# When a layer's input features are loaded and summed at the start of an encoder kernel: x's loads behind later weights, its sums behind later value chunks, the narrow projection one chunk later, the first k-tile in halves

## The chip, the core and the metric

The kernel runs on one core of a Trainium2 chip. A core has TensorE (matrix products, called PE in the profile; its weight loads are PEld), VectorE (DVE), ScalarE (ACT), GpSimd (POOL) and SyncE (SP), which here only issues transfers. Sixteen DMA engines move data between the chip's main memory and the core's own. The metric is the time of one execution on the device in microseconds, lower is better; a measurement is the median of several runs.

## What is computed

One layer of a streaming encoder, in float32: 256 tokens of 2048 features. A mixer (retention and a gated delta rule, both from one projection `w_in` of the normalised input), cross-attention into 256 memory tokens, and an MLP, with a residual addition after each and a final norm. What the change touches is the beginning of the work:

```
h = rms_norm(x, norm_mix_g)            # h1 in the kernel: input of every w_in projection
proj = h @ w_in                        # its 32 columns ga, gb give decays and betas of the delta rule
...
mem_n = rms_norm(mem, norm_mem_g)
k, v = split(mem_n @ w_xkv, 2)         # keys and values of the cross-attention
```

The norm of mem divides each token by a number of its own, so the kernel multiplies mem by the gain first, starts the products at once, and applies the per-token factor to the results later.

## The kernel before

Every product of two float32 matrices is made of three: each operand is split into a rounded part (hi, made by ScalarE with a copy into the narrower format) and a rest (lo, made by VectorE: the value less hi), and hi·hi + hi·lo + lo·hi are added up. So each piece of weights is loaded by a DMA into a `raw` buffer (three of them), cast to `whi` on ScalarE (L117) and `wlo` on VectorE (L118), half a megabyte at a time, and then used by TensorE. `fetch` (L95) does this; its instructions have a high priority. Activations are kept the same way, in quads of four k-tiles (128 features each): `memq` for mem, `h1` for the normalised x.

The kernel is written with a scheduler: it orders each engine's instructions by priority and data, when the program is built. On the chip each engine then runs its own list strictly in order, and a DMA is issued by the engine on whose list it stands. A transfer uses one of a few semaphores, and an issue waits until the earlier transfer that used the same one has landed.

The start of the program, in the order of the text:

- Eight calls of a matmul on ones warm TensorE up (L243, `WARM`). ScalarE issues the load of `gains` (L239), the gains of four norms.
- `values_both` (L363) makes the first two of four 512-column chunks of the values v together, k-tile by k-tile. Here block (q, n) is four k-tiles 4q to 4q+3 of chunk n; a block is 24 matmuls. For q = 0, `fetch_both` (L336) loads the weights in single k-tiles (L343), each with its k-tile of mem (L319), and casts them (L355, L358); `round_memory` splits mem times its gain into the quad, hi on ScalarE (L325), lo on VectorE (L326). For q = 1 to 3, mem is loaded by `load_memory` ahead of the block's weights, and rounded in the text behind the casts of the block's weights. TensorE's products are L370 to L372.
- `values(2)` and `values(3)` make the third and fourth chunk with the general `chunk` (L145, products L158 to L160). `keep_values` copies a result out of TensorE's memory (L333) and stores it.
- `narrow` (L211) makes the 32 columns of `w_in` with `h1`, 16 matmuls (L223), between the third and the fourth chunk, and `decay_rows` (L497) turns them into the decay rows `crow`, with a long chain of small VectorE instructions and some transposes on TensorE (L504, L544).
- Eight key blocks follow (L589 on, `blocks`, products L200 and L201), and beside them `rows_of`, `decays` and `ret_decays` prepare tables that the mixer reads later.

Beside this runs a generator `early` (L445), advanced by one `yield` for every two k-tiles of TensorE's products (`step`). The q = 0 blocks make steps 1 to 4, (1,0) 5 and 6, (1,1) 7 and 8, (2,0) 9 and 10, and so on to 16; the third chunk makes steps 17 to 24, the fourth 25 to 32. `behind()` (L79) orders what is traced inside it after the latest cast of weights on ScalarE and VectorE and after the latest load of weights on SP, if it runs on the same engine. Before the change `early` does the following: at steps 5 and 6 ScalarE issues the four loads of x (L452, half a megabyte each); at step 7 ScalarE issues `small` and `posi` (L456, L457); at steps 9 to 12 come the sums of squares of x (`norm_of`: squares on ScalarE L290, additions on VectorE L292 and L299, then the row of factors, which takes VectorE, GpSimd, TensorE and ScalarE in turn); at steps 13 to 20 `h1` (L468, L125, L126), one eighth a step; at steps 21 to 24 the sums of mem; then the rotations (VectorE, L413 to L441).

Of the kernel before, what the change touches and what calls it, by code (L numbers as in the profile page):

```python
# [17 lines left out]
P = 128  # L18
D = 2048
# [29 lines left out]
WARM = 8  # L49
# [3 lines left out]
def trunk(ctx: ExitStack, tc: tile.TileContext, x_f, mem_f, positions, gains_f, small_f, w_in, ret_gn_g, w_out, w_xq,  # L53
# [182 lines left out]
    with tc.high_priority(offset=300000):  # L236
        vec.memset(ones, 1.0)
        vec.memset(warm, 0.0)
        act.dma_start(gains, gains_f)  # L239
# [74 lines left out]
    mem_f32 = []  # L314

    def load_memory(c, ks):
        if ks.start == 0:
            mem_f32.append(kv.tile([P, 4, S], F32, name="xc", tag="xc", bufs=8))
        nc.sync.dma_start(mem_f32[c][:, ks], mem_f[:, 4 * c + ks.start:4 * c + ks.stop])  # L319

    def round_memory(c, ks):
        qh, ql = memq[c]
        for k in range(ks.start, ks.stop):
            g = gains[:, G_MEM + 4 * c + k:G_MEM + 4 * c + k + 1]
            act.activation(qh[:, k, :], mem_f32[c][:, k], AF.Copy, scale=g)  # L325
            vec.scalar_tensor_tensor(ql[:, k, :], mem_f32[c][:, k], g, qh[:, k, :].bitcast(F32),  # L326
                                     op0=ALU.mult, op1=ALU.subtract)
# [8 lines left out]
    def fetch_both():  # L336

        raws = [wp.tile([P, 2048], F32, name="raw", tag="raw", bufs=3) for _ in range(2)]
        got = []
        with tc.high_priority(offset=100000):  # L340
            for k in range(4):
                for n in range(2):
                    fetched.append(nc.sync.dma_start(raws[n][:, k * 512:(k + 1) * 512],  # L343
                                                     w_xkv[0, k * P:(k + 1) * P, D + n * 512:D + n * 512 + 512]).ins)
                    if not n:
                        load_memory(0, slice(k, k + 1))
            for h in range(2):
                tiles = [[wp.tile([P, 1024 + room], F32R, name=nm, tag=nm, bufs=3)[:, :1024]
                          for nm, room in (("whi", 64), ("wlo", 0))] for _ in range(2)]
                for k in range(2):  # L350
                    cs = slice(k * 512, (k + 1) * 512)
                    for n in range(2):
                        src = raws[n][:, (2 * h + k) * 512:(2 * h + k + 1) * 512]
                        hi, lo = (a[:, cs] for a in tiles[n])
                        latest["hi"] = act.activation(hi, src, AF.Copy).ins  # L355
                        if not n:
                            round_memory(0, slice(2 * h + k, 2 * h + k + 1))
                        latest["lo"] = vec.tensor_sub(lo, src, hi.bitcast(F32)).ins  # L358
# [4 lines left out]
    def values_both():  # L363
        pss = [stream_ps() for _ in range(2)]

        def products(n, kk, w, i):
            for t in range(NT):
                xh, xl = (a[:, kk % 4, t * P:(t + 1) * P] for a in memq[kk // 4])
                wh, wl = (a[:, i, :] for a in w)
# [823 lines left out]
```

## Time and profile before

| | |
|---|---|
| median of 3 runs | 2074.87 us (2074.64 to 2077.21) |
| the profiled execution | 2072.99 us |
| its span, first to last instruction | 2071.3 us |
| TensorE busy | 2057.7 us, 99% |
| VectorE busy | 1421.8 us, 69% |
| ScalarE busy | 1096.4 us, 53% |
| moved by DMA | 405.09 MB, mean 196 GB/s |

The page's second part cuts the span into 40 slices of 52 us; this change lies in the first two. A group line gives source line, engine, operation, what is written and read, shape and count, then busy time and mean duration in ns, then the engine's idle time before it and what ended it. A timeline row gives start, duration, engine, line and tiles, and in brackets the idle time before; several alike are merged, with their count. "q" behind an engine's name is its instruction queue, where DMA issues stand. A row of the waits gives who waited for whom, the total, how often and the longest. A row of the windows gives the stretch, its length, the busy time and count of each engine, the granted clock, the mean share of the DMA engines and GB/s. In TensorE's rows a duration includes the way through the array, so successive matmuls overlap, and the distance of their starts is the better measure.

### The profile page before, as it was taken

The numbers are of one execution on the slowest core, as the hardware profiler recorded it, in microseconds if no ns is written. First come the engines' busy times: TensorE is split into PE (matmuls) and PEld (weight loads), VectorE is DVE, ScalarE is ACT, GpSimd is POOL, SyncE is SP. The second block draws the span as 40 slices with busy tenths as digits, with TensorE's granted clock in tenths as the row PEclk, the third lists the DMA queues.
The fourth block names the chain that finished last, engine by engine and source line by source line (L and its number), as shares of the span: only waits on it lengthen the run. The fifth ranks groups of instructions, "written<-read, shape, count | busy, mean of one in ns | idle before, by whom it ended". The sixth has DMA issues, their size and how long they took to land.

```text
span 2071.3 us, 28351 instructions
## 1 busy us (share of the span) xinstructions
PE 2057.7 (99%) x10952; PEld 1773.0 (86%) x10952; DVE 1421.8 (69%) x2259; ACT 1096.4 (53%) x1739; POOL 30.6 (1%) x37
## 2 busy tenths in 40 slices
PE   9999999999999999999999999999999999999998
PEld 7788888988888888888888899888888888888887
DVE  6967778779767875888567665776556556655654
ACT  6655764675456554755455555554444434434444
POOL 0000000000000000000000000000000000000000
PEclk9999999999999999999999999999999999999999
DMA  8688566556556565655567654688666556656654
GB/s 295 209 286 270 177 195 197 162 183 186 187 171 190 181 194 163 190 182 178 163 223 237 191 183 143 191 209 231 199 187 192 195 190 196 185 201 186 197 187 142
DMA packets 329078, 405.09 MB, mean 196 GB/s; under 512 B 35040, under 2 KB 239088, under 8 KB 328816
## 3 DMA queue, kind: packets, MB, share of 16 engines
q1 hardware_dynamic: 327648, 400.34, 61.9%
q10 hardware_dynamic: 1296, 2.95, 0.4%
q8 instruction: 85, 1.39, 0.3%
q14 instruction: 49, 0.40, 0.1%
HBM read 389.61 MB, written 11.55 MB: 194 GB/s over the span
## 4 chain that ended last, share of the span: by engine, by line
PE 97%; DMA 1%; DVE 1%; ACT 0%; issue 0%; SPq 0%; ACTq 0%; POOLq 0%; POOL 0%; DVEq 0%
PE s L200 33%; PE s L201 17%; PE s L159 13%; PE s L158 13%; PE s L160 13%; DMA raw<-w_xkv 1%; PE b L760 1%; PE b L667 1%; PE b L793 1%; PE b L130 0%; PE b L129 0%; PE b L131 0%; PE s L372 0%; PE s L370 0%; PE s L371 0%
## 5 line engine op out<-in xcount | busy, mean ns | idle before, releaser
L118 DVE TENSOR_TENSOR wlo<-raw,whi 128x1024 fp32r<-128x1024 f32 x696 | 850.8, 1223 | 496.8 <-ACT whi L117 489.3
L117 ACT ACTIVATE whi<-raw 128x1024 fp32r<-128x1024 f32 x696 | 736.8, 1060 | 702.3 <-PE s L160 349.6
L200 PE MATMUL s<-q,whi 128*128 128x512 f32 x3072 | 1057.1, 391 | 0.3 <-DVE q L1060 0.3
L201 PE MATMUL s<-q,wlo 128*128 128x256 f32 x3072 | 838.7, 281 | 0.4 <-DVE wlo L118 0.4
L200 PEld LDWEIGHTS s<-q,whi 128*128 128x128 f32 x3072 | 567.4, 188 | 110.2 <-DVE q L1060 0.5
L201 PEld LDWEIGHTS s<-q,wlo 128*128 128x128 f32 x3072 | 576.4, 188 | 13.5 <-DVE wlo L118 1.1
L159 PE MATMUL s<-wlo,q 128*128 128x512 f32 (+1 forms) x1200 | 470.2, 392 | 0.0
L160 PE MATMUL s<-whi,q 128*128 128x512 f32 (+1 forms) x1200 | 467.6, 390 | 0.0
L158 PE MATMUL s<-whi,q 128*128 128x512 f32 (+1 forms) x1200 | 427.8, 390 | 0.0
L158 PEld LDWEIGHTS s<-whi,q 128*128 128x128 f32 x1200 | 225.0, 188 | 47.2
L160 PEld LDWEIGHTS s<-whi,q 128*128 128x128 f32 x1200 | 225.4, 188 | 45.8
L159 PEld LDWEIGHTS s<-wlo,q 128*128 128x128 f32 x1200 | 225.5, 188 | 45.3
L207 ACT ACTIVATE bo<-s 128x256 f32<-128x256 f32 x192 | 72.7, 379 | 124.4 <-PE s L201 111.3
L208 DVE TENSOR_TENSOR bo<-bo,s 128x256 f32<-128x256 f32 x192 | 80.0, 417 | 44.5 <-ACT bo L207 44.2
L620 DVE SCALAR_TENSOR_TENSOR acc<-bo,small,acc 128x255 f32<-128x255 f32 (+1 forms) x144 | 66.8, 480 | 3.1 <-ACT acc L617 1.2
L729 DVE TENSOR_TENSOR pr<-lw,tw 32x31 f32<-32x31 f32 (+15 forms) x124 | 40.5, 326 | 7.9 <-DMA lw<-scr_l 5.8
L731 DVE TENSOR_TENSOR tw<-tw,pr 32x31 f32<-32x31 f32 (+15 forms) x124 | 40.6, 327 | 2.0
L1107 DVE SCALAR_TENSOR_TENSOR res<-s,rstd3q,res 128x512 f32<-128x512 f32 (+1 forms) x32 | 22.3, 735 | 11.9 <-PE s L160 11.9
L894 ACT ACTIVATE gth<-s 128x512 f32<-128x512 f32 x32 | 18.9, 591 | 17.9 <-PE s L160 15.2
L1094 DVE SCALAR_TENSOR_TENSOR hs<-bo 128x256 f32<-128x256 f32 x64 | 26.9, 421 | 1.1
L1097 DVE TENSOR_TENSOR q<-hs,q 128x256 fp32r<-128x256 f32 x64 | 26.7, 419 | 0.0
L370 PE MATMUL s<-whi,q 128*128 128x512 f32 x64 | 23.4, 410 | 3.2 <-ACT q L325 3.2
(307 smaller groups left out, 1176.4 us busy)
## 6 DMA issues: line engine op xcount, KB each, us to landing
raw<-w_in SPq DMA_DIRECT2D x143, 1024.0 KB
raw<-w_ff SPq DMA_DIRECT2D x128, 1024.0 KB
raw<-w_xkv SPq DMA_DIRECT2D x29, 1024.0 KB
raw<-w_out SPq DMA_DIRECT2D x16, 1024.0 KB
raw<-w_xq SPq DMA_DIRECT2D x16, 1024.0 KB
raw<-w_xo SPq DMA_DIRECT2D x16, 1024.0 KB
dec_d<-dec_w SPq DMA_DIRECT2D x8, 384.0 KB
dec<-dec_d SPq DMA_DIRECT2D x8, 384.0 KB
```

Source lines behind the costliest of these rows:

```text
L117: latest["hi"] = act.activation(hi[:, cs], src[:, cs], AF.Copy).ins
L118: latest["lo"] = vec.tensor_sub(lo[:, cs], src[:, cs], hi[:, cs].bitcast(F32)).ins
L158: pe.matmul(o, xh, wh, start=first, stop=False)
L159: pe.matmul(o, xh, wl, start=False, stop=False)
L160: pe.matmul(o, xl, wh, start=False, stop=last)
L200: pe.matmul(ps[b], lh, xhl, start=kk == 0, stop=False)
L201: pe.matmul(ps[b][:, :S], ll, xh, start=False, stop=kk == KT - 1)
L207: act.activation(o, ps[b][:, S:], AF.Copy)
L208: vec.tensor_add(o, o, ps[b][:, :S])
L620: vec.scalar_tensor_tensor(acc[:, d:], ps[:, :S - d], cw[:, j, blk:blk + 1], acc[:, d:], op0=ALU.mult, op1=ALU.add)
L729: vec.tensor_mul(pv, lw[:, j, j + 1:32].unsqueeze(2).to_broadcast([32, n, j + 1]), tw[:, j, 0:j + 1].unsqueeze(1).to_broadcast([32, n, j + ...
L731: vec.tensor_sub(tw[:, j + 1:32, 0:j + 1], tw[:, j + 1:32, 0:j + 1], pv)
```

## The change

- **x's loads.** `early` yields eight times before it loads x, one chunk a step (steps 9 to 12), and SP issues the loads, `small` and `posi` as well (step 13), with a second load of mem's first k-tile, which the sums of mem need.
- **The sums.** Four more yields follow, so the sums of x come at steps 17 to 20, in the third value chunk, `h1` at steps 21 to 24, a quarter a step, the sums of mem at steps 25 to 28 and the rotations at step 29.
- **mem.** The loads of mem's third and fourth quad are traced behind the weights of blocks (1,1) and (2,0), and the rounding of a quad ahead of the block's fetch, behind the casts of the block before.
- **The first k-tile.** One load `lead`, issued by ScalarE, brings the gains and mem's first k-tile together. VectorE makes that k-tile's hi part (`first_q`). The first 512 columns of weights are loaded, cast and multiplied in two halves of 256. `WARM` is 6 instead of 8. The gains are copied from `lead` to their own tile later.
- **The narrow projection** comes behind the fourth chunk. `rows_of` moves into the third key block, and `decays` are spread over the key blocks from the fourth on.
- `trimask` is made in place, without `zer`.

```diff
@@ -46,11 +46,11 @@
-WARM = 8
+WARM = 6
...
@@ -236,7 +236,6 @@
     with tc.high_priority(offset=300000):
         vec.memset(ones, 1.0)
         vec.memset(warm, 0.0)
-        act.dma_start(gains, gains_f)
         act.activation(warm, warm, AF.Exp)
         early = bank()
         for _ in range(WARM):
@@ -312,19 +311,26 @@
     kv.tile([P, PAD1], F32, name="pad1", bufs=1)
     memq = [new_quad(kv, 4) for _ in range(4)]
     mem_f32 = []
+    lead = kv.tile([P, 64 + S], F32, name="lead", bufs=1)
+    mem_0 = lead[:, 64:]
+    with tc.high_priority(offset=400000):
+        act.dma_start(lead, lead_f)
+    with tc.high_priority(offset=300000):
+        first_q = vec.tensor_scalar(memq[0][0][:, 0, :], mem_0, lead[:, G_MEM:G_MEM + 1], None, op0=ALU.mult).ins
 
     def load_memory(c, ks):
-        if ks.start == 0:
+        if len(mem_f32) == c:
             mem_f32.append(kv.tile([P, 4, S], F32, name="xc", tag="xc", bufs=8))
-        nc.sync.dma_start(mem_f32[c][:, ks], mem_f[:, 4 * c + ks.start:4 * c + ks.stop])
+        return nc.sync.dma_start(mem_f32[c][:, ks], mem_f[:, 4 * c + ks.start:4 * c + ks.stop])
 
     def round_memory(c, ks):
         qh, ql = memq[c]
         for k in range(ks.start, ks.stop):
-            g = gains[:, G_MEM + 4 * c + k:G_MEM + 4 * c + k + 1]
-            act.activation(qh[:, k, :], mem_f32[c][:, k], AF.Copy, scale=g)
-            vec.scalar_tensor_tensor(ql[:, k, :], mem_f32[c][:, k], g, qh[:, k, :].bitcast(F32),
-                                     op0=ALU.mult, op1=ALU.subtract)
+            src = mem_f32[c][:, k] if c or k else mem_0
+            g = lead[:, G_MEM + 4 * c + k:G_MEM + 4 * c + k + 1]
+            if c or k:
+                act.activation(qh[:, k, :], src, AF.Copy, scale=g)
+            vec.scalar_tensor_tensor(ql[:, k, :], src, g, qh[:, k, :].bitcast(F32), op0=ALU.mult, op1=ALU.subtract)
 
     def keep_values(n, ps):
         vo = kv.tile([P, NT, 512], F32, name="vo", tag="vo", bufs=2)
@@ -337,25 +343,32 @@
 
         raws = [wp.tile([P, 2048], F32, name="raw", tag="raw", bufs=3) for _ in range(2)]
         got = []
+
+        def halves(n, k):
+            return ((0, 256), (256, 512)) if n == k == 0 else ((0, 512),)
+
         with tc.high_priority(offset=100000):
             for k in range(4):
                 for n in range(2):
-                    fetched.append(nc.sync.dma_start(raws[n][:, k * 512:(k + 1) * 512],
-                                                     w_xkv[0, k * P:(k + 1) * P, D + n * 512:D + n * 512 + 512]).ins)
-                    if not n:
+                    for c0, c1 in halves(n, k):
+                        at = D + n * 512
+                        fetched.append(nc.sync.dma_start(raws[n][:, k * 512 + c0:k * 512 + c1],
+                                                         w_xkv[0, k * P:(k + 1) * P, at + c0:at + c1]).ins)
+                    if n == 0 and k:
                         load_memory(0, slice(k, k + 1))
             for h in range(2):
                 tiles = [[wp.tile([P, 1024 + room], F32R, name=nm, tag=nm, bufs=3)[:, :1024]
                           for nm, room in (("whi", 64), ("wlo", 0))] for _ in range(2)]
                 for k in range(2):
-                    cs = slice(k * 512, (k + 1) * 512)
                     for n in range(2):
-                        src = raws[n][:, (2 * h + k) * 512:(2 * h + k + 1) * 512]
-                        hi, lo = (a[:, cs] for a in tiles[n])
-                        latest["hi"] = act.activation(hi, src, AF.Copy).ins
-                        if not n:
-                            round_memory(0, slice(2 * h + k, 2 * h + k + 1))
-                        latest["lo"] = vec.tensor_sub(lo, src, hi.bitcast(F32)).ins
+                        for c0, c1 in halves(n, 2 * h + k):
+                            src = raws[n][:, (2 * h + k) * 512 + c0:(2 * h + k) * 512 + c1]
+                            hi, lo = (a[:, k * 512 + c0:k * 512 + c1] for a in tiles[n])
+                            latest["hi"] = act.activation(hi, src, AF.Copy).ins
+                            if n == 0 and c0 == 0:
+                                round_memory(0, slice(2 * h + k, 2 * h + k + 1))
+                            with tc.issue_after(first_q):
+                                latest["lo"] = vec.tensor_sub(lo, src, hi.bitcast(F32)).ins
                 got.append([[a.rearrange("p (k n) -> p k n", n=512) for a in pair] for pair in tiles])
         latest["raw"] = fetched[-1]
         return got
@@ -363,29 +376,34 @@
     def values_both():
         pss = [stream_ps() for _ in range(2)]
 
-        def products(n, kk, w, i):
+        def products(n, kk, w, i, c0=0, c1=512):
             for t in range(NT):
+                o = pss[n][t][:, c0:c1]
                 xh, xl = (a[:, kk % 4, t * P:(t + 1) * P] for a in memq[kk // 4])
-                wh, wl = (a[:, i, :] for a in w)
-                pe.matmul(pss[n][t], xh, wh, start=kk == 0, stop=False)
-                pe.matmul(pss[n][t], xh, wl, start=False, stop=False)
-                pe.matmul(pss[n][t], xl, wh, start=False, stop=kk == KT - 1)
+                wh, wl = (a[:, i, c0:c1] for a in w)
+                pe.matmul(o, xh, wh, start=kk == 0 and c0 == 0, stop=False)
+                pe.matmul(o, xh, wl, start=False, stop=False)
+                pe.matmul(o, xl, wh, start=False, stop=kk == KT - 1)
 
         for h, both in enumerate(fetch_both()):
             for k in range(2):
                 for n in range(2):
-                    products(n, 2 * h + k, both[n], k)
+                    for c0 in (0, 256) if h == k == n == 0 else (0,):
+                        products(n, 2 * h + k, both[n], k, c0, c0 + 256 if h == k == n == 0 else 512)
                 step()
         for q in range(1, 4):
             for n in range(2):
+                if q == 1 and not n:
+                    with tc.high_priority(offset=100000):
+                        for ks in (slice(0, 2), slice(2, 4)):
+                            load_memory(1, ks)
                 if not n:
-                    with tc.high_priority(offset=100000):
-                        for ks in (slice(0, 2), slice(2, 4)) if q == 1 else (slice(0, 4),):
-                            load_memory(q, ks)
+                    with tc.high_priority(offset=100000), behind():
+                        round_memory(q, slice(0, 4))
                 halves = fetch(cols(w_xkv[0], D + n * 512)(q), 4, 512, cuts=1 if n or q > 1 else 2)
-                if not n:
-                    with tc.high_priority(offset=100000):
-                        round_memory(q, slice(0, 4))
+                if q + n == 2:
+                    with tc.high_priority(offset=100000), behind():
+                        load_memory(2 if n else 3, slice(0, 4))
                 for k in range(4):
                     products(n, 4 * q + k, halves[k // 2], k % 2)
                     if k % 2:
@@ -443,20 +461,23 @@
     scales = []
 
     def early():
-        for _ in range(4):
+        yield
+        with behind():
+            vec.tensor_copy(gains, lead[:, :64])
+        for _ in range(7):
             yield
         xfs = []
         for c in range(4):
             xfs.append(kv.tile([P, 4, S], F32, name="xc", tag="xc", bufs=8))
             with behind():
-                act.dma_start(xfs[c], x_f[:, 4 * c:4 * c + 4])
-            if c % 2:
-                yield
+                nc.sync.dma_start(xfs[c], x_f[:, 4 * c:4 * c + 4])
+            yield
         with behind():
-            act.dma_start(small, small_f)
-            act.dma_start(posi, positions[0].partition_broadcast(P))
-        yield
-        yield
+            nc.sync.dma_start(small, small_f)
+            nc.sync.dma_start(posi, positions[0].partition_broadcast(P))
+            load_memory(0, slice(0, 1))
+        for _ in range(4):
+            yield
         for got in norm_of("n1", xfs):
             yield
         for c in range(4):
@@ -469,7 +490,7 @@
                                                  gains[:, G_MIX + 4 * c + k:G_MIX + 4 * c + k + 1], got[1],
                                                  op0=ALU.mult, op1=ALU.mult)
                     split([a[:, 2 * k2:2 * k2 + 2, :] for a in h1[c]], xn)
-                yield
+            yield
         for got in norm_of("nm", mem_f32):
             yield
         scales.extend(got)
@@ -477,9 +498,8 @@
             rotations()
 
     trimask = kv.tile([P, P], F32, name="trimask", bufs=1)
-    zer = kv.tile([P, P], F32, name="zer", bufs=1)
-    vec.memset(zer, 0.0)
-    pool.affine_select(trimask, zer, pattern=[[1, P]], compare_op=ALU.is_ge, fill=-BIG, base=0, channel_multiplier=-1)
+    vec.memset(trimask, 0.0)
+    pool.affine_select(trimask, trimask, pattern=[[1, P]], compare_op=ALU.is_ge, fill=-BIG, base=0, channel_multiplier=-1)
 
     dist = kv.tile([P, S], F32, name="dist", bufs=1)
     pool.iota(dist, pattern=[[1, S]], base=0, channel_multiplier=-1, allow_small_or_imprecise_dtypes=True)
@@ -580,11 +600,10 @@
     steps.append(early())
     values_both()
     values(2)
-    narrow(h1, w_in[0], C_GA, 32, decay_rows)
     values(3)
     finish_steps()
     rstdm, mrow = scales
-    row4 = [rows_of(g) for g in range(4)]
+    narrow(h1, w_in[0], C_GA, 32, decay_rows)
 
     for b2 in range(8):
         ko = kv.tile([P, 2, S], F32, name="ko", tag="vo", bufs=2)
@@ -595,7 +614,9 @@
         blocks(memq, w_xkv[0], b2 * 256, 2, evac_k)
         nc.sync.dma_start(kt_d[:, 2 * b2:2 * b2 + 2, :], ko)
         with behind():
-            for h2 in ((), (), (0, 1), (2,), (3,), (4,), (5,), (6, 7))[b2]:
+            if b2 == 2:
+                row4 = [rows_of(g) for g in range(4)]
+            for h2 in ((), (), (), (0, 1), (2,), (3, 4), (5,), (6, 7))[b2]:
                 decays(h2)
             ret_decays(b2)
     kvs.close()
@@ -1174,8 +1195,9 @@
         arrays[name] = np.ascontiguousarray(inputs[name])
     arrays["x_f"] = _by_feature(inputs["x"][0])
     arrays["mem_f"] = _by_feature(inputs["mem"][0])
-    arrays["gains_f"] = np.concatenate([_by_feature(inputs[n])[:, :, 0] for n in
-                                        ("norm_mem_g", "norm_mix_g", "norm_x_g", "norm_ffn_g")], axis=1)
+    arrays["lead_f"] = np.concatenate([_by_feature(inputs[n])[:, :, 0] for n in
+                                       ("norm_mem_g", "norm_mix_g", "norm_x_g", "norm_ffn_g")]
+                                      + [arrays["mem_f"][:, 0]], axis=1)
     small = np.zeros((P, 323), np.float32)
     small[:, 0:192] = _by_feature(inputs["conv_w"][0]).transpose(0, 2, 1).reshape(P, 192)
     small[:, 192:320] = inputs["gdn_norm_g"][0]
```

More of the change, by code (lines that the diff above doesn't have):

```diff
@@ L48, with trunk @@
 MAGIC = 1.5 * 2.0**23
-WARM = 8
+WARM = 6
 @with_exitstack
-def trunk(ctx: ExitStack, tc: tile.TileContext, x_f, mem_f, positions, gains_f, small_f, w_in, ret_gn_g, w_out, w_xq,
+def trunk(ctx: ExitStack, tc: tile.TileContext, x_f, mem_f, positions, lead_f, small_f, w_in, ret_gn_g, w_out, w_xq,
           w_xkv, w_xo, w_ff1, w_ff2, norm_final_g, out):
```

## The prediction

> **What bounds the kernel now.** I read the page first, for who is busy, then TensorE's waits, then the timeline around the one long wait.
>
> ```profile
> span 2071.3 us, 28351 instructions
> PE 2057.7 (99%) x10952; PEld 1773.0 (86%) x10952; DVE 1421.8 (69%) x2259; ACT 1096.4 (53%) x1739; POOL 30.6 (1%) x37
> ```
>
> TensorE is idle for 13.6 of 2071.3 us. Nothing off TensorE can be worth more than a few us, and the question is only which of its idle time goes. Its waits, longest first:
>
> ```profile
> PE s L370 <- ACT q L325: 3.2, 2, 2.9
> PE b L243 <- DVE warm L238: 1.1, 1, 1.1
> PE s L201 <- DVE wlo L118: 0.4, 1, 0.4
> PE s L372 <- DVE q L326: 0.4, 1, 0.4
> ```
>
> One wait stands out: L370, the value products, for features of mem that ScalarE rounds (L325). On TensorE's timeline (start, duration):
>
> ```profile
> 28.25 0.40 PE L372 MATMUL s<-whi,q 128*128 128x512 f32 x1
> 31.57 0.50 PE L370 MATMUL s<-whi,q 128*128 128x512 f32 x1 [2.92 <-ACT q L325]
> 31.91 0.40 PE L371 MATMUL s<-wlo,q 128*128 128x512 f32 x1
> 32.37 0.40 PE L371 MATMUL s<-wlo,q 128*128 128x512 f32 x1
> 33.20 0.73 PE L372 MATMUL s<-whi,q 128*128 128x512 f32 x2 [0.43 <-DVE q L326]
> 33.78 0.39 PE L370 MATMUL s<-whi,q 128*128 128x512 f32 x1
> ```
>
> Starts tell more than durations, because matmuls overlap. Undisturbed 512-column matmuls start 0.23 us apart. Here the steps are 3.32, 0.34, 0.83 and, for the last two together, 0.58: too long by 3.09 + 0.11 + 0.60 + 0.12 = 3.9 us. This is the start of block (2,0), the third group of k-tiles. What ScalarE did before it:
>
> ```profile
> 16.52 1.31 ACTq L452 DMA_DIRECT2D xc<-x_f  x3
> 25.35 0.33 ACTq L456 DMA_DIRECT2D small<-small_f  x1
> 25.72 0.44 ACTq L457 DMA_DIRECT2D posi<-positions  x1
> 26.27 2.01 ACT L117 ACTIVATE whi<-raw 128x1024 fp32r<-128x1024 f32 x2 [4.36 <-PE s L372]
> 28.18 2.93 ACT L290 ACTIVATE sq<-xc 128x1024 f32<-128x1024 f32 x3
> 31.02 1.69 ACT L325 ACTIVATE q<-xc,gains 128x256 fp32r<-128x256 f32 x4
> ```
>
> ScalarE works in order. It idled 4.36 us to 26.27. The row names TensorE, but in ScalarE's own order stand the two DMA issues of 25.35 and 25.72, and L117 also needs the weights of (2,0); then it cast those weights, then squared three chunks of x (2.93 us), and only then rounded the mem features that TensorE was waiting for. The chain of waits has the weights, and the windows and queue rows say why they were late:
>
> ```profile
> 14.45 10.88 DMA raw<-w_xkv
> ```
> ```profile
> 17.00:28.30 11.30, 11.30 (x50) 9.02 (x49) 5.91 (x8) 5.40 (x8) 0.00 (x0) 1.00 1.04 401
> ```
> ```profile
> 38.00:40.00 2.00, 2.00 (x10) 1.64 (x9) 2.00 (x5) 1.06 (x1) 0.00 (x0) 1.00 0.05 17
> ```
> ```profile
> q10 hardware_dynamic: 1296, 2.95, 0.4%
> ```
>
> Issued at 14.45, landed at 25.33. All 16 DMA engines were full (share 1.04, 401 GB/s), and ten us later they were idle (0.05). The second queue, q10, carries what ScalarE issues: 2.95 MB, of which 2.1 are the four x chunks, in flight just then. At 401 GB/s they take 5.2 us of all DMA engines.
>
> **The change part by part.**
>
> *x to SP, behind the weights.* The x loads leave step 5 (after weights (1,0)) for steps 9 to 12, so in SP's order they stand behind weights (2,0). Of the 5.2 us, between half (two queues sharing) and all lay ahead of (2,0): it lands at 20.1 to 22.7 instead of 25.33. With four roundings (1.69) and a cast (half of 2.01) it is ready by 25.5, and TensorE comes for it at 28.5: 3 us of cover. small and posi no longer stand in ScalarE's queue, and the squares move to steps 17 and 18, in the third value chunk. All three causes go. Term: **-3.9**.
>
> *What is late next.* Behind x on SP stand weights (2,1) and (3,0); TensorE waits for those. From 22.7, mem 3 (0.5 MB), two x chunks (1.05) and weights (2,1) (1.05) take 6.5 us at 401 GB/s: 29.2, cast by 31.5 (one L117 and L118, 2.3), needed 5.6 us (24 x 0.233) after 28.5, at 34.1. Weights (3,0) with two more x chunks: 34.4, cast 36.7, needed 39.7. Cover 2.6 and 3.0 us, each lost one for one beyond that. SP issues seven DMAs more, at 0.33 to 0.47 us each as above, and SP has time, but it also waits:
>
> ```profile
> SPq L104 <- DVE wlo L118: 14.9, 4, 5.6
> SPq L104 <- DMA xc<-x_f: 8.6, 2, 6.8
> ```
>
> Before too, weight issues waited 8.6 us for x to land, without any later stall of TensorE. I take 0; the upper bound is in rival D.
>
> The Trainium skill, "DMA: Bandwidth & Descriptors", section Issuing engines are not separate DMA queues, speaks against this part: whoever issues, all DMAs run on the same 16 engines, so a change of issuer saves only issue time. The full windows agree (401 GB/s with both queues); by that rule alone the change would give 0. I hold that it is the order that gains.
>
> *First k-tile.*
>
> ```profile
> 1.10 3.78 PE L243 MATMUL b<-ones 128*128 128x128 f32 x16 [1.10 <-DVE warm L238]
> ```
> ```profile
> 5.20 1.22 PE L370 MATMUL s<-whi,q 128*128 128x512 f32 x2 [0.32 <-ACT q L325]
> 6.22 0.81 PE L371 MATMUL s<-wlo,q 128*128 128x512 f32 x2
> 6.86 0.63 PE L372 MATMUL s<-whi,q 128*128 128x512 f32 x2
> 8.49 0.40 PE L372 MATMUL s<-whi,q 128*128 128x512 f32 x1
> 8.78 0.73 PE L370 MATMUL s<-whi,q 128*128 128x512 f32 x2
> ```
> ```profile
> 4.12 0.63 ACT L355 ACTIVATE whi<-raw 128x512 fp32r<-128x512 f32 x1 [1.40 <-DMA raw<-w_xkv]
> 7.70 0.64 ACT L355 ACTIVATE whi<-raw 128x512 fp32r<-128x512 f32 x1 [1.06 <-DMA raw<-w_xkv]
> 8.23 0.49 ACT L325 ACTIVATE q<-xc,gains 128x256 fp32r<-128x256 f32 x1
> ```
>
> The first product waits for cast (0.63) and rounding (0.49) one after the other on ScalarE. Now VectorE rounds while ScalarE casts half a tile (about 0.4, an estimate from 0.63 for twice as much): first matmul near 4.6 instead of 5.20. But the second k-tile starts at 8.78, when its features are rounded (8.23 + 0.49 = 8.72), behind weights that landed at 7.70. The bytes ahead of those weights are the same as before (the gains and the first mem tile travel as one load). So the 0.6 us turns into waiting ahead of 8.78: term **0**. Bounds: gain up to 1.1 (ScalarE's wait of 1.06 before 7.70 vanishes), loss up to 1.3 (rival B). I take 0, nearest to the 8.23 row. Two 256-column matmuls for one 512-column one add at most some hundredths each, in the same slack.
>
> *Narrow projection.*
>
> ```profile
> L223 PE MATMUL s<-q,whi 128*64 128x512 f32 x16 | 3.8, 392 | 0.0
> L544 PE MATMUL b<-ident,xr 16*128 16x16 f32 x6 | 0.7, 216 | 0.0
> ```
>
> Its 16 matmuls move with their DMA, cast and decay chain from behind the third chunk to behind the fourth; the same 3.7 us are paid there. The loads of the decay rows come up to three key blocks later and the first calls of decays() one; its last four (h2 4 to 7) stay in the blocks where they were. They are needed only after the key blocks. Term 0; half a us either way, most of the 0.7 that six of the chain's transposes take in TensorE's stream.
>
> *Sums and h1 on VectorE.* The same instructions, later and denser: h1 gets four steps instead of eight.
>
> ```profile
> L118 DVE TENSOR_TENSOR wlo<-raw,whi 128x1024 fp32r<-128x1024 f32 x39 | 47.4, 1222 | 21.5 <-ACT whi L117 21.2
> L292 DVE TENSOR_TENSOR sq<-sq 128x1024 f32<-128x1024 f32 x6 | 7.3, 1220 | 0.6 <-ACT sq L290 0.5
> L468 DVE SCALAR_TENSOR_TENSOR xn<-xc,gains,n_row 128x256 f32<-128x256 f32 x16 | 6.8, 476 | 1.1 <-ACT n_row L283 1.1
> L126 DVE TENSOR_TENSOR q<-xn,q 128x512 fp32r<-128x512 f32 x8 | 5.3, 683 | 0.2 <-ACT q L125 0.2
> ```
> ```profile
> 56.00:78.20 22.20, 22.20 (x97) 17.81 (x96) 21.11 (x30) 15.85 (x20) 0.00 (x0) 1.00 0.59 180
> ```
>
> The third chunk (22.4 us) then holds 8 casts (9.8), x's sums (3.7, and about 1 for the two small ones, an estimate by size) and h1 (12.1): 26.6, over by 4.2. The casts have priority, so the surplus should slide into the fourth chunk, which holds casts, mem's sums and the 18 steps of the rotations (at most 8.6, at L468's 0.476 each): 23.1, and what is left slides into the key blocks, since only h1 has to be ready for narrow, and it comes first. The row above shows VectorE 95% full while TensorE was 100% busy. I take 0.
>
> **Sum:** -3.9. Against the profiled execution (2072.99 us, 1.7 of it around the span): 2069.1. The median before is 2074.87, 1.9 above that execution, so I forecast 2074.87 - 3.9 = **2071.0**.
>
> **The rivals.**
> - A, the start gains too: the second k-tile's weights land sooner. For it: ScalarE waited 1.06 us for them. Against: equal bytes ahead. 0.5 to 1.1 more: 2070.1.
> - B, TensorE reaches full speed later. Starts were 0.41 to 0.6 us apart until about 6.6, then 0.23: slow until 5.5 us after the first warm-up matmul. Two warm-up calls fewer and a gap before 4.6 may push the step back. Twelve matmuls at 0.41 from 4.6 end at 9.5, 0.75 late against 8.78, and three more cold ones add 0.5: loss 0.7 to 1.3, so 2072.0. The Trainium skill, "TensorE: Matmul & The Clock Gate", Part 1, has a free-running window of about 3.4 us that must be busy: by that rule one more window would keep it cold to about 10, the upper price. The trace agrees that there is a step; one execution cannot show the window.
> - C, slower than before: VectorE becomes the bound in the third value chunk. If casts queue behind the h1 bundles in VectorE's fixed order, TensorE pays the surplus of 4.2, and if it pays what slides on as well (4.2 + 23.1 - 22.4 = 4.9), 9.1: -3.9 + 4.2 to 9.1, so 2075.2 to 2080.1. It decides once more than 3.9 us of surplus reach TensorE. Against it: the 95% row.
> - D, the change doesn't do what it says: x on SP keeps weights late, now (2,1) or (3,0), and the stall moves. If they come 5.2 us later than worked out, 2.6 is lost at (2,1): 2073.6; at full price 2074.9.
>
> **How the numbers follow.** Forecast 0.56, A 0.26, B 0.07, C 0.06, D 0.05. The range runs from A's full 1.1 and half a us of transposes on the base of the profiled execution (2072.99 - 3.9 - 1.1 - 0.5 = 2067.5) to 2074.0: B, the forecast on the slowest run before (2077.21 - 3.9 = 2073.3) and D's lower price lie inside, C and D's upper price outside. About 0.2%, 4.1 us, is what a measurement of this kernel tells from no change. The forecast lies right at it, and the terms that I set at 0 lean to gain at the start, so 0.30 of its 0.56 count as faster. Faster 0.30 + 0.26 = 0.56; same 0.26 + 0.07 + 0.05 and half of C, 0.41; slower the other half of C, 0.03.
>
> **What would show it.** Right: no wait of L370 for L325 beyond a few tenths, x_f issued by SP behind weights (2,0), L290 after 45 us, TensorE's matmuls 0.23 apart from 9 to 45 us. A: the second k-tile starts before 8.3. B: starts 0.41 apart after 7 us. C: waits of L158 to L160 for wlo between 45 and 90 us. D: a new wait for weights near 34 or 39 us. Wrong altogether: a stall after 110 us that wasn't there, for I cost nothing beyond the key blocks.

## The result and the profile after

| | before | after |
|---|---|---|
| median, runs side by side | 2074.02 us (2071.81 to 2077.21, 10 runs) | 2069.03 us (2068.66 to 2069.42, 10 runs) |
| the profiled execution | 2072.99 us | 2069.25 us |
| its span | 2071.3 us | 2067.5 us |

The ratio is 0.9975, with an interval of 0.9966 to 0.9985: the change gains 5.0 us where 3.9 were forecast. The two profiled executions are 3.7 us apart. So two questions stand: which part gained it, and where the 1.1 us between 3.9 and 5.0 come from.

The page's first lines, and TensorE's waits (who waited for whom, total, how often, longest):

```profile
span 2067.5 us, 28359 instructions
PE 2056.7 (99%) x10954; PEld 1773.0 (86%) x10954; DVE 1420.2 (69%) x2262; ACT 1096.9 (53%) x1739; POOL 30.7 (1%) x37
```
```profile
PE b L242 <- DVE warm L238: 1.1, 1, 1.1
PE s L201 <- DVE wlo L118: 1.0, 1, 1.0
PE s L384 <- DVE q L319: 0.4, 1, 0.4
PE s L200 <- DVE q L1081: 0.3, 1, 0.3
```

The wait of 3.2 us of the value products (L370 before, L384 now) is gone, and no new one of its size has come. The 1.0 of L201 lies at the start of the mixer (204 us), where before had 0.4; x5, before unchanged, has 0.7 and x9 0.9, so it isn't read as an effect. TensorE at the start of block (2,0), start and duration:

```profile
28.17 0.40 PE L386 MATMUL s<-whi,q 128*128 128x512 f32 x1
28.40 0.63 PE L384 MATMUL s<-whi,q 128*128 128x512 f32 x2
28.86 0.40 PE L385 MATMUL s<-wlo,q 128*128 128x512 f32 x1
```

Starts are 0.23 us apart right through the place where before stood still from 28.5 to 31.6. Why, ScalarE's timeline shows:

```profile
22.33 1.69 ACT L332 ACTIVATE q<-xc,lead 128x256 fp32r<-128x256 f32 x4
24.41 1.06 ACT L117 ACTIVATE whi<-raw 128x1024 fp32r<-128x1024 f32 x1 [0.38 <-DMA raw<-w_xkv]
...
30.96 2.01 ACT L117 ACTIVATE whi<-raw 128x1024 fp32r<-128x1024 f32 x2 [4.10 <-DMA raw<-w_xkv]
...
36.23 2.01 ACT L117 ACTIVATE whi<-raw 128x1024 fp32r<-128x1024 f32 x2 [1.66 <-DMA raw<-w_xkv]
...
49.16 1.04 ACT L289 ACTIVATE sq<-xc 128x1024 f32<-128x1024 f32 x1
```

The features of block (2,0) are rounded from 22.33 to 24.02 (before: from 31.02), ahead of its weights; those are cast from 24.41, and the squares (L289) come at 49.16. The weights of the next two blocks end a wait of ScalarE at 30.96 and 36.23, 1.8 later each than the 29.2 and 34.4 that the prediction had worked out, and still 3.0 and 3.4 us ahead of the blocks that use them (first matmuls at 34.00 and 39.60). On SP's queue x (L473) now stands behind those of (2,0), two chunks ahead of the weights of (2,1) and two behind them:

```profile
14.32 0.37 SPq L104 DMA_DIRECT2D raw<-w_xkv  x1
...
16.20 1.14 SPq L473 DMA_DIRECT2D xc<-x_f  x2
19.50 0.38 SPq L104 DMA_DIRECT2D raw<-w_xkv  x1
19.93 0.98 SPq L473 DMA_DIRECT2D xc<-x_f  x2
```

In time that is a smaller step than in the program's text: before, ScalarE issued all four chunks from 16.52 on, also after the weights of (2,0) (14.45), but ahead of those of (2,1) (19.85).

The windows (length, busy time of PE, PEld, DVE, ACT, POOL, granted clock, DMA share, GB/s) and the second queue's row:

```profile
28.30:33.90 5.60, 5.60 (x26) 4.51 (x25) 1.84 (x2) 2.94 (x5) 0.00 (x0) 1.00 1.03 395
38.00:40.00 2.00, 2.00 (x10) 1.64 (x9) 1.74 (x3) 0.33 (x2) 0.00 (x0) 1.00 1.02 379
```
```profile
q10 hardware_dynamic: 432, 0.69, 0.1%
```

At 38 to 40 us, where the DMA engines were idle before (0.05), they are now full (1.02): the bytes of x haven't become fewer, they lie later, in time that stood empty. q10 has fallen from 2.95 to 0.69 MB.

### The profile page after: what moved, and what is told of

Read it like the earlier page. It is cut to its first block, busy times and chain, and to the rows that moved or that the text cites. A ratio compares the mean times of both kernels' runs of the same rounds, so it can differ in the third digit from the quotient of the medians.

```text
span 2067.5 us, 28359 instructions
## 1 busy us (share of the span) xinstructions
PE 2056.7 (99%) x10954; PEld 1773.0 (86%) x10954; DVE 1420.2 (69%) x2262; ACT 1096.9 (53%) x1739; POOL 30.7 (1%) x37
## 4 chain that ended last, share of the span: by engine, by line
PE 99%; DVE 0%; issue 0%; ACT 0%; DMA 0%; POOLq 0%; POOL 0%; ACTq 0%
PE s L200 34%; PE s L201 18%; PE s L159 13%; PE s L158 13%; PE s L160 13%; PE s L384 1%; PE s L386 1%; PE s L385 1%; PE b L781 1%; PE b L688 1%; PE b L814 1%; PE b L130 0%; PE b L129 0%; PE b L131 0%; PE b L690 0%; PE b L686 0%
## 5 line engine op out<-in xcount | busy, mean ns | idle before, releaser
L201 PE MATMUL s<-q,wlo 128*128 128x256 f32 x3072 | 837.5, 281 | 1.0 <-DVE wlo L118 1.0
L201 PEld LDWEIGHTS s<-q,wlo 128*128 128x128 f32 x3072 | 576.4, 188 | 14.9 <-DVE wlo L118 1.7
L160 PE MATMUL s<-whi,q 128*128 128x512 f32 (+1 forms) x1200 | 467.4, 390 | 0.0
L158 PE MATMUL s<-whi,q 128*128 128x512 f32 (+1 forms) x1200 | 427.5, 390 | 0.0
L158 PEld LDWEIGHTS s<-whi,q 128*128 128x128 f32 x1200 | 225.0, 188 | 47.2
L160 PEld LDWEIGHTS s<-whi,q 128*128 128x128 f32 x1200 | 225.4, 188 | 45.7
L1117 ACT ACTIVATE q<-hs 128x256 fp32r<-128x256 f32 x64 | 26.1, 409 | 0.6 <-DVE hs L1115 0.6
```

What stands on the lines that cost most here:

```text
L158: pe.matmul(o, xh, wh, start=first, stop=False)
L160: pe.matmul(o, xl, wh, start=False, stop=last)
L201: pe.matmul(ps[b][:, :S], ll, xh, start=False, stop=kk == KT - 1)
```

## The experiments

Each ran beside kernel before on its chip. Those made from before keep before's line numbers.

**The first four ask which part gains.** x1 changes the issuer alone, at the old place:

```diff
-                act.dma_start(xfs[c], x_f[:, 4 * c:4 * c + 4])
+                nc.sync.dma_start(xfs[c], x_f[:, 4 * c:4 * c + 4])
...
-            act.dma_start(small, small_f)
+            nc.sync.dma_start(small, small_f)
```

> The kernel before, with one difference: the loads of x, small and posi are issued by SP instead of ScalarE, at the same steps 5 to 7, and the sums stay where they were. Theory 1 (order: x's 2.1 MB stand ahead of weights (2,0), and the squares ahead of the rounding of mem): nothing is gained by the issuer, TensorE still stalls 3 to 6 us near 28 us, time within 0.1% of before or up to 0.2% above. Rival (issuer: it is the DMA issues on ScalarE's list that hold the casts back): the stall falls below 1 us and the time by 3 us or more.

Measured: 2073.31 us (2072.44 to 2077.09) against 2074.56; ratio 0.9995 (0.9986 to 1.0004). The waits, and ScalarE:

```profile
PE s L370 <- ACT whi L117: 2.4, 1, 2.4
```
```profile
24.19 2.00 ACT L117 ACTIVATE whi<-raw 128x1024 fp32r<-128x1024 f32 x2 [5.81 <-DMA raw<-w_xkv]
```

The stall has only moved, to block (1,1) at 22.5 us: now that block's weights come late. The edit moved the issue in time too: SP issues x from 10.34 us on, ahead of those weights (12.89), where ScalarE did from 16.52. So x1 shows that SP as the issuer is not enough for a gain; x9 below asks for the issuer alone. The Trainium skill, "DMA: Bandwidth & Descriptors", section Issuing engines are not separate DMA queues, says that a change of issuer saves only the time of issuing, and this ratio agrees with it; what gains is decided by the next two.

x2 leaves the loads of x as they were and makes only the sums, h1 and narrow late:

```diff
-        yield
+        for _ in range(9):
+            yield
...
-    narrow(h1, w_in[0], C_GA, 32, decay_rows)
     values(3)
     finish_steps()
     rstdm, mrow = scales
-    row4 = [rows_of(g) for g in range(4)]
+    narrow(h1, w_in[0], C_GA, 32, decay_rows)
...
```

> The kernel before, with x loaded as before (ScalarE, steps 5 and 6), but the sums of x, h1, the sums of mem and the rotations at the changed kernel's steps (17 on), and the narrow projection behind the fourth chunk. Theory 1 splits its stall: the weights (2,0) still land near 25 us, but behind their two casts the rounding of mem follows at once (28.2 us instead of 31.0), so most of the stall goes: 0.3 to 1 us is left, time 2.9 to 3.6 us less. Rival (late transfers alone make the stall): 2 us or more are left, and the time falls by less than 2 us.

Measured: 2071.14 us (2070.62 to 2074.57); ratio 0.9985 (0.9976 to 0.9994).

```profile
PE s L370 <- ACT q L325: 0.8, 3, 0.3
...
PE s L371 <- DVE wlo L118: 0.5, 1, 0.5
```

With the squares out of ScalarE's way, 3.4 us come; short waits for rounding and for late weights are left.

x3 has x's loads on SP at the new steps as well, but the old first k-tile and the old order of mem:

```diff
-        for _ in range(4):
+        for _ in range(8):
             yield
...
-                act.dma_start(xfs[c], x_f[:, 4 * c:4 * c + 4])
-            if c % 2:
-                yield
+                nc.sync.dma_start(xfs[c], x_f[:, 4 * c:4 * c + 4])
+            yield
...
```

> The kernel before with the changed kernel's x part (loads by SP at steps 9 to 12, sums from step 17) and its narrow projection, but the old first k-tile, the old warm-up and mem's loads and roundings in the old order. Theory 1: this is nearly all of the change: the wait of L370 for L325 near 28 us is under 0.3 us, time 3.5 to 5 us less, about as the changed kernel. Rival (the start makes part of the 5 us): at least 1 us is missing against the changed kernel.

Measured: 2069.30 us (2069.07 to 2070.01); ratio 0.9975 (0.9964 to 0.9985), the same as the whole change. So the place of x's loads gives the other 1.8 us (x2's fastest run, 2070.62, is slower than x3's slowest), and the rest of the change has nothing left to give that these runs can tell. Two things come earlier in x3's profile than in x2's: the rounding for (2,0) (17.42 instead of 27.97, ahead of that block's casts) and the weights of (2,1) (cast from 29.69 instead of 34.02). How the 1.8 us divide between them is not shown. x4 confirms it from the other side, with the first k-tile alone (lead, halves, `first_q`, `WARM` 6) and x, sums and narrow as before:

```diff
-WARM = 8
+WARM = 6
...
+    lead = kv.tile([P, 64 + S], F32, name="lead", bufs=1)
...
+            vec.tensor_copy(gains, lead[:, :64])
...
```

> The kernel before with the changed kernel's first k-tile alone (one load of gains and mem's first k-tile, half tiles, VectorE's rounding, 6 warm-up calls); x, sums, mem order and narrow as before. Theory 1: first matmul near 4.4 us, but the second k-tile starts at 8.5 to 8.8 us as before; the stall near 28 us stays at 3 to 4 us or grows by the time gained at the start; time within 0.5 us of before. Rival (the start gains): 1 us or more less.

Measured: 2075.28 us (2073.12 to 2078.74); ratio 1.0003 (0.9995 to 1.0012). On TensorE:

```profile
7.74 0.40 PE L386 MATMUL s<-whi,q 128*128 128x512 f32 x1
8.74 0.73 PE L384 MATMUL s<-whi,q 128*128 128x512 f32 x2 [0.59 <-ACT q L332]
```

The first k-tile is done sooner, and TensorE waits 0.59 us until the second one's features are rounded: 8.74, where before had 8.78.

**Then the size.** After their stalls x4 and x1 have matmuls 0.43 us apart for a while (x4 only from 33.5 us on, after 1.5 us at 0.23), where before's profiled execution soon has 0.23 again. The theory formed on this: the stall often costs TensorE its clock as well, and before's profiled execution is one in which it didn't. Its rival: profiled executions are simply shorter, and the 1.1 us are scatter of the median. x5 is before unchanged, profiled once more.

> The kernel before, unchanged, for one more profile. Of 30 runs of it, 28 show a mean clock of 0.998 or 0.997, and only 2 show 0.999 as in the profile that the prediction was made from. Theory 2 (the stall has a second price: TensorE's clock falls to half after it): this profile shows the stall near 28 us, and behind it matmuls 0.43 us apart for about 3.4 us, a span of 2072 to 2074 us. Rival (the 5 us come from waits alone, and longer ones than in that profile): a stall of 5 us and no slow matmuls.

It took 2073.95 us. TensorE's timeline, and three windows of it:

```profile
28.11 0.40 PE L372 MATMUL s<-whi,q 128*128 128x512 f32 x1
31.41 0.65 PE L370 MATMUL s<-whi,q 128*128 128x512 f32 x1 [2.91 <-ACT q L325]
31.86 0.63 PE L371 MATMUL s<-wlo,q 128*128 128x512 f32 x1
32.29 0.63 PE L370 MATMUL s<-whi,q 128*128 128x512 f32 x1
...
34.93 0.44 PE L370 MATMUL s<-whi,q 128*128 128x512 f32 x1
35.21 0.39 PE L371 MATMUL s<-wlo,q 128*128 128x512 f32 x1
```
```profile
28.20:31.40 3.20, 0.30 (x2) 0.00 (x0) 2.62 (x4) 3.20 (x5) 0.00 (x0) 1.00 1.05 389
31.61:35.02 3.41, 3.41 (x9) 2.39 (x9) 3.41 (x6) 3.41 (x9) 0.00 (x0) 0.50 1.05 387
35.02:38.43 3.41, 3.41 (x16) 2.77 (x15) 3.41 (x7) 2.19 (x4) 0.00 (x0) 1.00 0.68 249
```

The wait is the same (2.91 us, before 2.92), but from 31.61 the granted clock is 0.50 for 3.41 us, and nine matmuls run where sixteen run afterwards. From 31.41 to 35.21 nine steps take 3.80 us instead of 9 x 0.233 = 2.10: 1.7 lost. In before's profiled execution it was 0.11 + 0.60 + 0.12 = 0.8 in the same place. The difference, 0.9, is the one between the two executions (2073.95 - 2072.99 = 0.96).

That it is the rule rather than the exception is shown by the mean clock of every run. A stretch of 3.41 us at half clock lowers it by 3.41 x 0.5 / 2072 = 0.0008. The 72 runs of kernel before beside these experiments:

| mean granted clock | runs | median (from, to) |
|---|---|---|
| 0.999 | 8 | 2072.79 us (2072.39 to 2073.35) |
| 0.998 | 54 | 2074.56 us (2072.97 to 2076.87) |
| 0.997 | 10 | 2076.07 us (2075.37 to 2077.24) |

By this measure eight runs in nine lose one stretch or more; the medians of the rows lie 1.8 and then 1.5 us apart, more than the 0.96 between the two profiled executions. All ten runs of after have 0.999, and so have all of x3, x8, x9 and x10; none of x4 and x7 has.

x6 tests the cause: kernel before, its wait untouched, with 13 calls of a matmul on ones in it. Their results are not used.

```diff
+                if q == 2 and not n:
+                    filler = bank()
+                    with tc.issue_after(latest_pe["mm"]):
+                        for _ in range(13):
+                            fill = pe.matmul(filler[:, :P], ones, ones, start=True, stop=True).ins
...
```

> The kernel before, with 13 calls of a matmul on ones (26 matmuls, 2.9 us at full speed) put between the blocks (1,1) and (2,0), so that TensorE works while it waits; their result is not used, and the stall itself is not touched. Theory 2: the wait stays as long as it was, but the clock stays up: mean clock 0.999 in nearly all runs, a scatter of less than 2 us, time 1 to 1.7 us less than before. Rival (waits alone): same time as before within 0.3 us, same scatter.

Measured: 2073.36 us (2072.33 to 2075.33) against 2074.66; ratio 0.9996 (0.9987 to 1.0005). The mean clock is 0.999 in 10 of 11 runs (kernel before beside it: 4 of 25). TensorE's timeline and a window:

```profile
28.68 0.40 PE L373 MATMUL s<-whi,q 128*128 128x512 f32 x1
28.92 3.06 PE L394 MATMUL b<-ones 128*128 128x128 f32 x26
32.37 0.50 PE L371 MATMUL s<-whi,q 128*128 128x512 f32 x1 [0.39 <-ACT q L325]
32.71 0.39 PE L372 MATMUL s<-wlo,q 128*128 128x512 f32 x1
```
```profile
32.37:35.78 3.41, 2.96 (x12) 2.12 (x13) 3.41 (x6) 3.41 (x8) 0.00 (x0) 1.00 1.05 389
```

The real products start later than in before (32.37 against 31.57), yet the clock stays at 1.00 and the median falls by 1.3 us. The interval of the time alone takes in no change; it is the clock, in 10 runs of 11, that shows it: here TensorE loses its clock because it has nothing to do, not because of what it waits for.

x7 moves narrow and the decays alone:

```diff
-    narrow(h1, w_in[0], C_GA, 32, decay_rows)
     values(3)
     finish_steps()
...
+    narrow(h1, w_in[0], C_GA, 32, decay_rows)
...
```

> The kernel before, with only the narrow projection behind the fourth chunk and the later loads and calls of the decay tables. The prediction gave this part 0, half a us either way. Theory: within 0.5 us of before, no new wait of TensorE. Rival: it gives some of what was measured beyond 3.9 us, 0.5 to 1.1 us less.

Measured: 2075.03 us (2073.88 to 2077.32); ratio 1.0002 (0.9993 to 1.0011): nothing, as the term said. Its profiled execution is its longest (2077.32 us) and shows the second size of the loss:

```profile
PE s L370 <- ACT q L325: 5.4, 3, 4.6
```
```profile
32.71:39.54 6.83, 5.72 (x14) 4.37 (x15) 6.73 (x12) 5.94 (x12) 0.00 (x0) 0.50 0.83 306
```

After a wait of 4.6 us the clock was at half for 6.83 us, twice 3.41. The edit lies far behind this place, so the wait itself seems not to be the same in every execution either: 2.9 us in both profiles of before, 4.6 here.

x8 is after with the warm-up of before, `WARM = 8`, for rival B.

> The changed kernel with 8 warm-up calls instead of 6. The prediction gave 6 calls a loss of 0 to 1.3 us (its case B). Theory: the second k-tile starts at 8.6 to 8.8 us whatever the warm-up does, time within 0.3 us of the changed kernel, so 4.7 to 5.3 us less than before. Rival (case B in part): 0.5 us or more faster than the changed kernel.

Measured: 2069.36 us (2068.31 to 2070.18); ratio 0.9974 (0.9964 to 0.9983), after's own. TensorE at the start of x8, then of after:

```profile
4.53 0.77 PE L384 MATMUL s<-whi,q 128*128 128x256 f32 x2
...
6.97 0.73 PE L384 MATMUL s<-whi,q 128*128 128x512 f32 x2 [0.47 <-ACT whi L367]
...
8.73 0.62 PE L384 MATMUL s<-whi,q 128*128 128x512 f32 x2
```
```profile
4.39 0.77 PE L384 MATMUL s<-whi,q 128*128 128x256 f32 x2 [0.36 <-DVE q L319]
...
7.09 0.70 PE L384 MATMUL s<-whi,q 128*128 128x512 f32 x2
...
8.68 0.73 PE L384 MATMUL s<-whi,q 128*128 128x512 f32 x2
```

**The last two ask what of the x part is needed.** x9 is x3 with ScalarE as the issuer (`act.dma_start` in place of `nc.sync.dma_start`, for `small` and `posi` too):

> As the kernel of x3 (x at steps 9 to 12, sums from step 17, narrow behind the fourth chunk, old first k-tile), but ScalarE issues the loads of x, small and posi, as before the change. Theory 1 (order, not issuer): no stall near 28 us over 0.5 us, clock 0.999, time within 0.5 us of x3, so 4.5 to 5.5 us less than before. Rival (the issuer counts too: issues on ScalarE's list wait for a free semaphore and hold the casts behind them): 1 us or more lost against x3, with idle time of ScalarE ahead of L117 behind an issue.

Measured: 2070.61 us (2069.04 to 2072.22) against 2074.50; ratio 0.9980 (0.9971 to 0.9989). ScalarE:

```profile
25.95 0.82 ACTq L452 DMA_DIRECT2D xc<-x_f  x2
...
39.88 1.71 ACT L325 ACTIVATE q<-xc,gains 128x256 fp32r<-128x256 f32 x4 [1.68 <-DMA xc<-mem_f]
```

No stall at 28 us either, whoever issues. But ScalarE issues x only where its list of casts lets it (the first at 25.95; SP in after: 16.20), the last quad of mem lands later, and its rounding at 39.88 makes TensorE wait 0.7 us. Its median is 1.3 above x3's, where theory 1 expected at most 0.5; they ran on different chips and the intervals overlap, so neither that size nor the rival is settled.

x10 is x3 with the sums at steps 14 to 17 and h1 in eight steps behind them:

```diff
             nc.sync.dma_start(posi, positions[0].partition_broadcast(P))
-        for _ in range(4):
-            yield
+        yield
...
```

> As the kernel of x3, but the sums of x follow right behind its loads, at steps 14 to 17, and h1 in eight steps from 18. Theory 1: once x lands behind the weights, the place of the sums costs little, since a block's rounding of mem is no longer late: within 0.7 us of x3. Rival (the squares on ScalarE are a cause of their own): a stall of 1 us or more at the start of block (3,0) or (3,1), near 39 to 45 us, and as much lost.

Measured: 2069.54 us (2068.69 to 2070.09) against 2074.50; ratio 0.9974 (0.9963 to 0.9985). With x loaded at steps 9 to 12, the sums may come three steps sooner at no cost that the measurement can tell. The medians of x3, x8 and x10 are within 0.6 us of after's; no version tried beats it.

## Why the prediction was right, and in what it was not

**The mechanism was right in the main.** All signs that were named came: no wait of the value products for the rounding, x issued by SP behind weights (2,0), the squares at 49.16, matmuls 0.23 us apart. The split wasn't in the prediction: 3.4 us come when the squares leave ScalarE's list (x2), the other 1.8 when x's loads move as well (x3); neither cause is all of it.

**The term of -3.9 was right for the execution that it was read from:** 2072.99 to 2069.25 is 3.74, and the sum against the profiled execution, 2069.1, lies 0.15 beside what was measured.

**The step that was mis-sized** is the last of the sum, "The median before is 2074.87, 1.9 above that execution, so I forecast 2074.87 - 3.9". It took those 1.9 us over to the changed kernel as if they had nothing to do with the stall. About half were the stall's second price. By x5 the stall costs 3.30 - 0.23 = 3.07, and the half clock 1.7: 4.8, not 3.9, in an execution that loses one stretch; before's ten-run median less that is 2074.02 - 4.8 = 2069.2, against 2069.03. Beside the experiments before's medians were 2074.5 to 2074.7 and x3 and x8 gained 5.3; these last 0.5 us are not taken apart. The other part was the base: the three runs shown had a median 0.85 above that of ten. Together, 1.1 + 0.85 is the 2.0 us between 2071.0 and 2069.03. One thing was there to be doubted: three runs that spread over 2.6 us, with the profiled execution below all three. The loss of the scatter fits this too: after's ten runs lie within 0.8 us, before's within 5.4.

**When (2,0) is ready** was forecast well by luck, because two errors cancel. Its weights ended a wait at 24.41, only 0.9 us sooner than before's 25.33, where 20.1 to 22.7 were worked out. The step that failed is "between half (two queues sharing) and all lay ahead of (2,0)", 2.6 to 5.2 us. x9 has the measure of it: there no x was in flight before 25.95, and these weights still took from 13.82 to 23.28, 9.5 us, where before took 10.88. By that comparison x's bytes cost them about 1.4 us, an estimate, for mem's loads lie in other places there too. The second error made up for it: the features were already rounded by 24.02, before the cast and not after it, so that the hi half of the first weights was there at 25.47 (forecast 25.5), 2.9 us before TensorE came for it at 28.40.

**Rival A:** not seen. The second k-tile starts at 8.68 (8.78 before), and x4 gains nothing: the 0.6 us did turn into waiting, as the forecast had it. **Rival B:** the later step is seen, but it isn't shown to be the warm-up's. In after, with six calls, the 256-column matmuls run at half pace until 7.09 (starts 0.21 apart), in x8, with eight, until about 5.4 (then 0.12). But x4, also with six, has the step at 6.2, before, with eight, at 6.6, and x9, with eight, at 7.04 by its clock record: it differs between executions by as much. x8 then waits 0.47 us for a cast at 6.97 and reaches the second k-tile at 8.73. Whatever moves the step, the loss lies in slack, and x8's time says the same. **Rival C:** no wait of L158 to L160 for a cast from 45 to 90 us. But VectorE didn't work as forecast there. The windows of after's third and fourth chunk and of the first key products, and h1's row (min/median/max ns, first and last start):

```profile
50.80:74.08 23.28, 23.28 (x106) 18.93 (x104) 14.40 (x14) 13.85 (x16) 0.70 (x1) 1.00 0.64 204
74.08:96.91 22.83, 22.83 (x102) 18.48 (x100) 21.94 (x37) 14.72 (x20) 0.71 (x1) 1.00 0.57 173
96.91:104.00 7.09, 7.09 (x40) 5.46 (x39) 5.69 (x13) 4.16 (x7) 0.00 (x0) 1.00 0.96 293
```
```profile
L489 DVE SCALAR_TENSOR_TENSOR xn<-xc,gains,n_row x16: 475/481/490, 75.9 to 100.2; 128x256 f32<-128x256 f32 x16
```

The third chunk holds 14.4 us of VectorE's work, not 26.6; the fourth holds 21.9 of 22.8 (forecast 23.1, before what slides on). h1 starts at 75.9 only, behind x's sums and their row of factors, and ends after 100, when the key blocks have begun. "It comes first" was wrong; the price, 0, was right, because TensorE has key products to do meanwhile. **Rival D:** no stall near 34 or 39 us. The weights were 1.8 us later than worked out and used that much of the covers of 2.6 and 3.0: 0.8 and 1.2 us are left, by the forecast's way of counting. x1 shows what happens when x stands further forward: the cover is gone and the stall is back, 2.4 us.

**Why one wait takes the clock and another doesn't** can be read from the clock records of the traces. In each, the first record of full clock comes a few us after the start (before 6.59, x1 4.84, x4 6.12, x5 4.30, x7 5.40), and the half clock of x1, x4, x5 and x7 sets in exactly six or eight times 3.413 us after it. So the time may be cut into cells of that length. These are the two cells of before over which its wait is spread, and the cells of x4 and x1 ahead of their half clock (the second number is TensorE's busy time):

```profile
27.07:30.48 3.41, 1.57 (x7) 0.94 (x5) 2.64 (x3) 3.41 (x5) 0.00 (x0) 1.00 1.03 393
30.48:33.89 3.41, 1.89 (x7) 1.27 (x8) 3.31 (x6) 3.41 (x7) 0.00 (x0) 1.00 1.06 392
```
```profile
30.02:33.43 3.41, 1.19 (x4) 0.67 (x4) 2.83 (x5) 3.41 (x7) 0.00 (x0) 1.00 1.05 388
```
```profile
21.91:25.32 3.41, 1.03 (x6) 0.50 (x4) 0.05 (x1) 1.13 (x2) 0.00 (x0) 1.00 1.03 398
```

The cells that cost the clock have 1.19 (x4), 1.03 (x1), about 0.5 (x5) and 0 us (x7) of busy TensorE; before's two, with 1.57 and 1.89, kept it. So in these five executions the clock went by how the wait lay on the cells, not by its length alone, and that differs from one execution to the next. It explains x4 too, where the clock falls 1.5 us after the work has begun again. The Trainium skill, "TensorE: Matmul & The Clock Gate", Part 1, tells of a free-running window of 3413 ns after which an idle TensorE is put to half clock. The stretches of 3.41 and 6.83 us at 0.50 and the cells agree with it. Its section HAM oscillation — how this bites in real kernels gives gaps of more than about 3.4 us as those that bite; here 2.91 us (x5) and 2.4 us (x1) were enough, in cells that were not wholly idle, so the measurement sets the bound lower.

**What stays open:** where between 1.19 and 1.57 us of busy time the bound lies; it is read from five profiled executions, and no run placed the wait on purpose. Nor is it shown why the waits themselves differ (2.9 us in before, 4.6 in x7).

## What to carry to other kernels

Waits of TensorE of 2.4 us and more were not priced here by their own length alone: look at the distance of the starts and the granted clock in the few us behind it, and at the mean clock of all runs, not only of the profiled one. Where the median lies above the profiled execution, ask whether the thing being removed makes the difference, before carrying it over. Large loads that are needed late belong behind the weights that are needed next, in the order in which they are issued: issued by another engine, but sooner, they only moved a stall from one block to the next (x1).

## What was not expected of the hardware

After a wait of 2.4 to 4.6 us TensorE's granted clock was 0.50 for 3.41 us (x1, x4, x5) or 6.83 us (x7), and 512-column matmuls started 0.43 us apart instead of 0.23. In kernel before, 64 of 72 runs had a mean clock that shows it. 26 small matmul instructions in the wait (x6) left a mean clock of 0.999 in 10 runs of 11, against 4 of 25 of kernel before beside it. At the very start the matmuls run at this same half pace while the windows of the profile give the clock as 1.00, because the clock record begins only with the full clock (5.21 us in x8, 7.22 in after); there the distance of the starts is the sign.
